# Two seven-product units on one NeuronCore: two of four weight sums of the second unit move from accumulating transfers to VectorE

## The chip, the core and the metric

The kernel runs on one core of a Trainium2 chip. The core has five engines that run side by side, each with its own queue of instructions worked off in order, and they wait for each other through semaphores. TensorE (PE in the profile) multiplies, with its weight loads shown apart as PEld. VectorE (DVE), ScalarE (ACT) and GpSimd (POOL) do elementwise work. SyncE (SP) only issues transfers here. Transfers are issued from SP's, ACT's and POOL's queues and carried by 16 DMA engines. The metric is the time of one execution in device microseconds (us); lower is better.

## The reference, cut to what matters

One decoder layer on 512 tokens with a model width of 1024: a layer norm, a token mixer (gated linear attention, called GLA, beside multi-head latent attention, called MLA), a merge by sigmoid gates, an output projection, and an MLP with hidden width 4096.

```python
h = layer_norm(x, ln_in_g, ln_in_b)
q_g, k_g, v_g, r_g, a_lr, q_lat, kv_lat, gate_logits = jnp.split(h @ w_in, offsets, axis=-1)
o_gla = gla_chunked(q_g, k_g, v_g, log_a)             # 4 heads, 256 values each
y_gla = (rms_norm(o_gla, gla_norm_g) * silu(r_g)) @ w_o_gla
y_mla = mla_causal_attention(...) @ w_o_mla           # 8 heads
g_gla, g_mla = split(sigmoid(gate_logits + b_gate))
h = layer_norm(ALPHA * h + (g_gla * y_gla + g_mla * y_mla) @ w_out, ln1_g, ln1_b)
out = layer_norm(ALPHA * h + square(relu(h @ w_ff1)) @ w_ff2, ln2_g, ln2_b)
```

The change lies in `v_g = h @ w_in[:, 1024:2048]` and `r_g = h @ w_in[:, 2048:3072]`, two products of 512x1024 by 1024x1024, and in the place where a GLA head's output is multiplied by silu of `r_g`.

## The kernel before

All products use float32 operands split in two parts, a high one (rounded to the type fp32r) and a low one (what is left), and each product of two blocks is three matmuls: high by high, high by low, low by high. A weight tile is split in `pump` (lines 165 to 189): ScalarE copies the raw tile into `whi` or `xh` (line 185), and VectorE subtracts that from the raw tile into `wlo` or `xl` (line 186). A table called `stream` lists every weight tile of the program in the order of use; `pump` keeps the transfers two tiles and the splits one or two tiles ahead of the product that TensorE is on. The pair `whi`/`wlo` has two buffers each, so a split into them waits until TensorE is done with the tile two uses earlier; `xh`/`xl` lie in a larger pool of 4 KB buffers (called A here).

The products for `r_g` and `v_g` are done by `unit` with seven products instead of eight. A 1024x1024 weight is cut in four blocks 11, 12, 21, 22 of 512x512. Seven products, here called phases 0 to 6, use the weights T1, 11, 22, T2, 21, T3 and T4, where T1 = 11 + 12, T2 = T1 + 22, T3 = 22 + 12 and T4 = T2 + 21 (signs are put on the other factor). The other factor is a block of `h`, or a sum of such blocks, called S1 to S4, which is computed once in the first unit (`r`), kept in device memory, and fetched again by POOL's queue for the second unit (`v`). Each phase has two half phases of 12 matmuls with a 512-wide right side, one for each tile of two rows of 128.

The four weight sums are made by transfers: `r_load` loads a block into a tile called `rw` (512 KB), and with `add` it issues a transfer from POOL's queue that adds another block onto the tile. T2 is added onto the tile of T1 once T1 has been split, and T4 onto T2 in the same way; T3 is added onto the tile of 22. `r_begin` issues T1's two loads and its two adds. For the unit `v` this is called from the middle of the unit `r`.

Between the matmuls of the units, small pieces of other work are woven in by `tick`: the GLA heads' decay levels (the tiles `M`, `qk`, `SD`, `tot`, `pr` and `qkp`; a head's `tot`, `pr` and `qkp` are made by POOL, and `tot` then passes through ScalarE before VectorE multiplies `qk` by it), and silu of the unit `r`'s result (`th` by ScalarE, then a multiply by VectorE at line 725, then a store `rd` to device memory). After the unit `v` come the gates' products (line 236 to 238), among which the GLA heads' outputs are made by `gla_out`; it fetches a head's part of silu(`r_g`) back as a tile `rg`.

The program's text gives priorities, not the final order: a scheduler of the framework puts each engine's instructions in an order of its own, by priority and by when it reckons each can start. So a moved call moves rows on several queues.

Of the kernel before, what the change touches and what calls it, by code (L numbers as in the profile page):

```python
# [52 lines left out]
def tile_hybrid_block(ctx: ExitStack, tc: tile.TileContext, I, out, dbg=None):  # L53
# [19 lines left out]
    def A(shape, dt=F32, n="a"):  # L73
        tag, bufs = ("C", 8) if n in TAG_C else (n, TAG_W[n]) if n in TAG_W else ("A", 24)
        return pa.tile(shape, dt, tag=tag, bufs=bufs, name=nm(n))
# [86 lines left out]
    def pump(i):  # L162
        while st["dma"] < min(len(stream), i + 1 + DMA_AHEAD):
            e = stream[st["dma"]]
            st["dma"] += 1
            if "src" in e:
                continue
            raw = A([P, e["nk"], T * 2 // e["nk"]], F32, "wraw")
            for sl, src, cw in e["dmas"]:
                dst = raw[:, sl, :e["n"]]  # L170
                if cw is not None:
                    dst = dst.rearrange("p (h c) -> p h c", c=cw)
                nc.sync.dma_start(dst, src)
            e["raw"] = raw
        while st["spl"] < min(len(stream), i + 2 + SPLIT_AHEAD):
            e = stream[st["spl"]]
            if st["spl"] > i + e.get("ahead", SPLIT_AHEAD) and not e["res"]:
                break
            nk, n = e["nk"], e["n"]
            hi, lo = [A([P, nk, T * 2 // nk], F32R, w) for w in HOME["a" if e["res"] else e.get("home", "w")]]  # L180
            raw = e["src"]() if "src" in e else e.pop("raw")
            with ExitStack() as gates:
                for g in st["gates"]:
                    gates.enter_context(tc.issue_after(g.ins))
                st["ins"] = act(hi[:, :nk, :n], raw[:, :nk, :n], AF.Copy)  # L185
                vtt(lo[:, :nk, :n], raw[:, :nk, :n], f(hi[:, :nk, :n]), op=ALU.subtract)  # L186
            st["gates"] = ()
            e["w"] = (hi, lo)
            st["spl"] += 1

# [101 lines left out]
    PL["k"] = plan("w_in", C_K, T)  # L292
    ORDER = (("r", 0), ("v", 0), ("g", 0), ("g", 2), ("qr", 0), ("g", 1), ("g", 3), ("qr", 1))

    RPH = ("T1", "11", "22", "T2", "21", "T3", "T4")
    RW = {}
    RAHEAD, RHOME = 2, {"r": "wawawawawawaww", "v": "wawawawawawaww"}
# [4 lines left out]
    for sec, i in ORDER:  # L302
        if sec in "rv":
            c0 = {"r": C_R, "v": C_V}[sec]
            for n, op in enumerate(RPH):
                for hf in range(2):
                    PL[sec, n, hf] = len(stream)
                    if op in ("11", "21"):
                        plan("w_in", c0, T, 4 * (op == "21") + 2 * hf, 4 * (op == "21") + 2 * hf + 2)
                    else:  # L310
                        stream.append({"src": lambda q=(sec, op, hf): RW[q], "nk": 2, "n": T, "res": False})
                    stream[-1].update(ahead=RAHEAD, home=RHOME[sec][2 * n + hf])
        elif sec == "g":
            PL["g", i // 2, i % 2] = plan("w_in", C_G + i * T, T)
        else:
            plan_qr(i)
# [299 lines left out]
    def r_begin(sec):  # L616
        for hf in range(2):
            r_load(sec, "T1", 0, 1, hf)
        r_add(sec, "T1", "T1", 0, 0)

    def r_add(sec, dst, src, i, j):
        for hf in range(2):
            RW[sec, dst, hf] = RW[sec, src, hf]
            r_load(sec, dst, i, j, hf, add=True)
# [8 lines left out]
    def fetch(name):  # L633
        RS[name] = [A([P, 4, 256], F32R, name) for _ in range(2)]
        for d, w in zip(KEPT[name], RS[name]):
            nc.gpsimd.dma_start(w, d)
# [63 lines left out]
    def unit(sec, nxt=None):  # L700
# [45 lines left out]
        for n in range(7):  # L746
            o = a if n in (1, 3, 5) else b
            for hf in range(2):
                pump(PL[sec, n, hf])
                for pp in range(2):  # L750
                    for t in range(2):
                        xh, xl = lhs(n, 2 * hf + pp, t)
                        hi, lo = [w[:, pp] for w in stream[PL[sec, n, hf]]["w"]]
                        opens = n in (0, 1, 4, 6) and hf == 0 and pp == 0
                        mm(o[t], xh, hi, start=opens, stop=False, skip_group_check=True)
                        mm(o[t], xh, lo, start=False, stop=False, skip_group_check=True)
                        mm(o[t], xl, hi, start=False, stop=hf == 1 and pp == 1, skip_group_check=True)
                if hf == 0 and (val or n in (0, 2, 4, 6)):
                    tick(None)
                if n == 0 and hf == 1:  # L760
                    r_add(sec, "T2", "T1", 1, 1)
                    if val:
                        fetch("S2")
                if n == 2 and hf == 1:
                    r_add(sec, "T3", "22", 0, 1)
                    if val:
                        fetch("S3")
                if n == 3 and hf == 1:
                    r_add(sec, "T4", "T2", 1, 0)
                if n == 5 and hf == 0 and nxt:  # L770
                    r_begin(nxt)
                    fetch("S1")
                    fetch("S4")
                if n == 6 and hf == 0 and nxt:
                    for h2 in range(2):
                        r_load(nxt, "22", 1, 1, h2)
            for t in range(2):
                if n == 0:
                    put("22", t, o[t], -1.0)
                elif n == 1:  # L780
                    put("11", t, o[t])
                elif n == 2:
                    put("12", t, o[t], -1.0)
                elif n == 3:
                    last("12", t, o[t], ALU.subtract)
                elif n == 4:
                    last("11", t, o[t], ALU.add)
                elif n == 5:
                    put("21", t, o[t])
                    last("22", t, o[t], ALU.subtract)  # L790
                else:
                    last("21", t, o[t], ALU.add)
            if n < 6:
                tick(None)
# [129 lines left out]
    def gla_out(h):  # L924
        while SS[h] is None or Vp[h // 2] is None or Rp[h // 2] is None:
            yield
        sd, s128, kq = SS[h]
        rg = A([P, NT, HV], F32, "rg")
        for i in range(2):
            nc.sync.dma_start(rg[:, 2 * i:2 * i + 2], Rp[h // 2][i][:, :, h % 2 * HV:(h % 2 + 1) * HV])  # L930

        def V(j):
            c = slice(h % 2 * HV, (h % 2 + 1) * HV)
# [12 lines left out]
        for i in range(NT):  # L946
# [12 lines left out]
                mm(o, al, bh, start=False, stop=n == len(todo) - 1)  # L959
            sq = B([P, HV], F32, "osq")  # L960
            act(sq, o, AF.Square, accum_out=ss[:, i:i + 1])
            if i >= 1:
                yield
        vts(ss, ss, 4.0 / HV, 4.0 * RMS_EPS, op0=ALU.mult, op1=ALU.add)
# [3 lines left out]
        og = [B([P, 2, HV], F32, "og") for _ in range(2)]  # L968
        for i in range(NT):
            o = ps[i // 2][:, (i % 2) * HV:(i % 2 + 1) * HV]  # L970
            stt(og[i // 2][:, i % 2, :], o, rs[:, i:i + 1], rg[:, i],
                op0=ALU.mult, op1=ALU.mult)
        yield
        for kk in range(2):
# [582 lines left out]
```

## Time and profile before

| What | Value |
| --- | --- |
| median of 3 runs | 883.69 us (883.59 to 885.77) |
| the profiled execution | 883.45 us, of which 881.7 us is the span from the first to the last instruction |
| mean granted TensorE clock | 0.994 |
| TensorE matmuls | 854.5 us busy, 97% of the span |
| VectorE, ScalarE, GpSimd | 69%, 53%, 21% busy |
| transfers | 127.35 MB, mean 144 GB/s |

A row of the profile that names a source line counts by the kernel before (L186 is line 186 of it). In a timeline, the bracket at a row's end says how long the engine was idle before it, and which engine or transfer ended that idle time. Rows of equal instructions that follow each other are merged, with their count. In a table of stretches, each engine's busy time stands with its instructions in brackets; "PEclk" is the granted clock as a share of full speed. Matmuls overlap: one with a 512-wide right side is shown with 0.39 us, while the next one starts 0.23 us after it.

### The profile page before, as it was taken

To read this page: it belongs to the slowest core of one execution; us is meant where nothing else is said; L and a number is where in the kernel's file an instruction comes from. 1 tells how busy PE (TensorE), PEld (TensorE's weight loads), DVE (VectorE), ACT (ScalarE), POOL (GpSimd) and SP (SyncE) were. 2 spreads that over 40 slices of the span, in tenths; PEclk is the share of its full clock that TensorE was granted. 3 is DMA by queue.
4 is the path that set the end of the run, shared out by engine and by line. 5 is a ranking of instruction groups with operands and counts; after the bars stand their busy time and mean duration, and the time that the engine had idled before them with its cause. 6 is when DMAs were issued, how large, how long until landed. Compare 5 with 4: busy or idle time off the path is not lost. (4 is left out here: it accounts for less than half of the span.)

```text
span 881.7 us, 11628 instructions
## 1 busy us (share of the span) xinstructions
PE 854.5 (97%) x4288; PEld 726.2 (82%) x4288; DVE 610.0 (69%) x993; ACT 466.2 (53%) x802; POOL 188.0 (21%) x221
## 2 busy tenths in 40 slices
PE   5999997999999999999999999999999999999995
PEld 5988785778898888888988888988888888888885
DVE  7977986796556344557876797886567556754697
ACT  5467765564554433435654414565457546735662
POOL 2404683603202010000000013004400520242023
PEclk9999998999999999999999999999999999999998
DMA  7836898933454223111307527006941990398075
GB/s 229 241 103 218 250 267 227 250 124 105 122 176 120 63 63 105 52 53 55 109 25 261 191 76 282 1 1 168 291 114 30 260 256 27 68 304 202 0 191 96
DMA packets 73240, 127.35 MB, mean 144 GB/s; under 512 B 8641, under 2 KB 34676, under 8 KB 73184
## 3 DMA queue, kind: packets, MB, share of 16 engines
q1 hardware_dynamic: 50848, 70.86, 24.8%
q0 software_dynamic: 20416, 52.11, 24.7%
q10 hardware_dynamic: 1920, 3.66, 1.2%
q8 instruction: 33, 0.54, 0.2%
q14 instruction: 23, 0.19, 0.1%
HBM read 99.86 MB, written 12.58 MB: 128 GB/s over the span
## 5 line engine op out<-in xcount | busy, mean ns | idle before, releaser
L186 DVE TENSOR_TENSOR wlo<-wraw,whi 128x1024 fp32r<-128x1024 f32 (+2 forms) x90 | 102.2, 1137 | 97.8 <-ACT whi L185 92.0
L236 PE MATMUL mm<-h,whi 128*128 128x512 f32 x416 | 163.2, 393 | 0.1
L237 PE MATMUL mm<-h,whi 128*128 128x512 f32 x416 | 162.8, 391 | 0.0
L238 PE MATMUL mm<-h,wlo 128*128 128x512 f32 x416 | 155.9, 391 | 0.1
L185 ACT ACTIVATE whi<-wraw 128x1024 fp32r<-128x1024 f32 (+2 forms) x90 | 87.0, 967 | 69.9 <-PE mm L237 34.5
L1419 POOL DMA_DIRECT2D res<-ev x54 | 47.8, 992 | 237.6 <-ACT ev L1417 194.2
L236 PEld LDWEIGHTS mm<-h,whi 128*128 128x128 f32 x416 | 78.2, 188 | 16.0 <-ACT whi L185 0.3
L238 PEld LDWEIGHTS mm<-h,wlo 128*128 128x128 f32 x416 | 77.9, 188 | 16.2 <-DVE wlo L186 0.5
L237 PEld LDWEIGHTS mm<-h,whi 128*128 128x128 f32 x416 | 78.2, 188 | 15.1
L1484 ACT ACTIVATE relu<-mm 128x512 f32<-128x512 f32 x32 | 18.8, 595 | 56.9 <-PE mm L238 56.9
L374 POOL TENSOR_TENSOR mv<-mv,mhalf 128x1 f32<-128x1 f32 x4 | 4.1, 1036 | 208.5 <-DVE mv L373 208.5
L185 ACT ACTIVATE xh<-wraw 128x1024 fp32r<-128x1024 f32 (+1 forms) x24 | 23.2, 974 | 26.8 <-PE mm L271 15.4
L614 POOL DMA_DIRECT2D rw<-in_w_in_dram x24 | 26.1, 1128 | 32.6 <-DVE xl L186 12.9
L186 DVE TENSOR_TENSOR wlo<-wq,whi 128x1024 fp32r<-128x1024 f32 x15 | 18.4, 1224 | 19.9 <-ACT whi L185 19.9
L856 ACT ACTIVATE M<-qk 128x256 f32<-128x256 f32 x56 | 23.9, 454 | 14.1 <-DVE qk L838 13.3
L186 DVE TENSOR_TENSOR xl<-wraw,xh 128x1024 fp32r<-128x1024 f32 (+1 forms) x24 | 27.0, 1137 | 6.3 <-ACT xh L185 6.3
L1417 ACT ACTIVATE ev<-mm 128x512 f32<-128x512 f32 x20 | 11.9, 600 | 31.6 <-DMA res<-ev 27.8
L838 DVE TENSOR_TENSOR qk<-qk,tot 128x512 f32<-128x512 f32 x28 | 23.5, 840 | 7.1 <-PE px L894 4.2
L1334 POOL DMA_DIRECT2D wq<-in_w_ff_dram x32 | 24.5, 1024 | 11.1 <-issue 4.6
L236 PE MATMUL mm<-ogT,whi 128*128 128x512 f32 x64 | 25.7, 401 | 0.0
L237 PE MATMUL mm<-ogT,whi 128*128 128x512 f32 x64 | 25.3, 395 | 0.0
L237 PE MATMUL mm<-omT,whi 128*128 128x512 f32 x64 | 25.2, 394 | 0.0
(457 smaller groups left out, 2413.6 us busy)
## 6 DMA issues: line engine op xcount, KB each, us to landing
wraw<-in_w_in_dram SPq DMA_DIRECT2D x32, 512.0 KB, 4.6
wraw<-in_w_ff_dram SPq DMA_DIRECT2D x32, 512.0 KB, 8.6
wq<-in_w_ff_dram POOLq DMA_DIRECT2D x32, 512.0 KB, 9.9
res<-ev POOLq DMA_DIRECT2D x54, 256.0 KB, 8.6
rw<-in_w_in_dram POOLq DMA_DIRECT2D x24, 512.0 KB, 7.7
S<-s SPq DMA_DIRECT2D x8, 512.0 KB, 6.4
S<-S POOLq DMA_DIRECT2D x8, 512.0 KB, 7.1
wraw<-in_w_o_gla_dram SPq DMA_DIRECT2D x8, 512.0 KB, 3.7
```

The source lines that it names most:

```text
L185: st["ins"] = act(hi[:, :nk, :n], raw[:, :nk, :n], AF.Copy)
L186: vtt(lo[:, :nk, :n], raw[:, :nk, :n], f(hi[:, :nk, :n]), op=ALU.subtract)
L236: mm(o, hi[:, c], xh, start=first, stop=False)
L237: mm(o, hi[:, c], xl, start=False, stop=False)
L238: mm(o, lo[:, c], xh, start=False, stop=last)
L614: nc.gpsimd.dma_start(RW[sec, op, hf], w[:, k0:k0 + 2, c0:c0 + T], **({"accum_op": ALU.add} if add else {}))
L838: vtt(new, new, view(tot, o + 1, -1, 2, 0, s), op=ALU.mult)
L856: act(packed(M, s, i), half_lr(qk, s, i), AF.Copy)
L1334: nc.gpsimd.dma_start(t, w2[:, k0:k0 + 3:2, j * T:(j + 1) * T])
L1417: st["ev"] = act(e, o, AF.Copy, scale=-1.0 if ph == 4 else 1.0)
L1419: nc.gpsimd.dma_start(res[tt + t][:, j * T:(j + 1) * T], e, accum_op=ALU.add)
L1484: act(r, ps, AF.Relu)
```

## The change

The unit `r` is left as it is. In the unit `v`, the sums T2 and T4 are no longer made by transfers that add onto the tile of T1. Instead `v_sum` lets VectorE add the raw tile of 22 onto the tile of T1, in place, right behind the split of 22, and the raw tile of 21 onto it right behind the split of 21. That is four additions of 128x1024 (two halves each), and four fewer accumulating transfers of 512 KB on POOL's queue. T1 = 11 + 12 and T3 = 22 + 12 are still made by transfers.

The start of the unit `v` (`r_begin`: two loads and two adds of T1) is called in phase 3 of the unit `r`, where it was called in phase 5. S1's fetch is called half a phase later than before, and S4's in phase 0 of the unit `v`, where it was called in phase 5 of the unit `r`.

In `gla_out`, silu(`r_g`) is fetched into two tiles of 2 KB a partition from another pool, after the head's third output block, where it was fetched into one tile of 4 KB ahead of all.

```diff
@@ pump @@
             st["gates"] = ()
+            if "then" in e:
+                e["then"](raw)
             e["w"] = (hi, lo)
@@ ahead of the stream of the two units @@
+    def v_sum(a, b, hf, raw):
+        t = RW["v", b, hf] = RW["v", a, hf]
+        vtt(t, t, raw, op=ALU.add)
+
@@ stream of the two units @@
                     stream[-1].update(ahead=RAHEAD, home=RHOME[sec][2 * n + hf])
+                    if sec == "v" and op in ("22", "21"):
+                        stream[-1]["then"] = lambda raw, a={"22": "T1", "21": "T2"}[op], b={"22": "T2", "21": "T4"}[op], hf=hf: v_sum(a, b, hf, raw)
@@ unit @@
                 if n == 0 and hf == 1:
-                    r_add(sec, "T2", "T1", 1, 1)
+                    if not val:
+                        r_add(sec, "T2", "T1", 1, 1)
                     if val:
                         fetch("S2")
...
-                if n == 3 and hf == 1:
+                if n == 3 and hf == 1 and not val:
                     r_add(sec, "T4", "T2", 1, 0)
-                if n == 5 and hf == 0 and nxt:
+                if n == 3 and hf == 0 and nxt:
                     r_begin(nxt)
+                if n == 5 and hf == 1 and nxt:
                     fetch("S1")
+                if n == 0 and hf == 0 and val:
                     fetch("S4")
@@ gla_out @@
-        rg = A([P, NT, HV], F32, "rg")
-        for i in range(2):
-            nc.sync.dma_start(rg[:, 2 * i:2 * i + 2], Rp[h // 2][i][:, :, h % 2 * HV:(h % 2 + 1) * HV])
...
+            if i == 2:
+                rg = []
+                for j in range(2):
+                    rg.append(B([P, 2, HV], F32, "rgb"))
+                    nc.sync.dma_start(rg[j], Rp[h // 2][j][:, :, h % 2 * HV:(h % 2 + 1) * HV])
...
-            stt(og[i // 2][:, i % 2, :], o, rs[:, i:i + 1], rg[:, i],
+            stt(og[i // 2][:, i % 2, :], o, rs[:, i:i + 1], rg[i // 2][:, i % 2],
```

What the scheduler makes of it is seen on two engines. The first is POOL, late in the unit `r`. In these rows of the kernel before, `qkp` and `tot` belong to GLA head 1, `rw_275_1396` and `rw_276_1398` are the two halves of the unit `v`'s T1, which appear first as loads and then as adds, and S1 and S4 are the fetches:

```order
L813 TENSOR_TENSOR tot_260_1309<-tot_260_1309 128x16
L813 TENSOR_TENSOR tot_260_1309<-tot_260_1309 128x8
L824 TENSOR_TENSOR qkp_263_1322<-pr_261_1319,qkp_262_1321 128x512
L813 TENSOR_TENSOR tot_260_1309<-tot_260_1309 128x4
L614 DMA rw_275_1396<-in_w_in_dram 128x2x512
L614 DMA rw_276_1398<-in_w_in_dram 128x2x512
L636 DMA S1_277_1402<-S1_136_714 128x1024
L636 DMA S1_278_1403<-S1_137_715 128x1024
L636 DMA S4_279_1406<-S4_167_876 128x1024
L636 DMA S4_280_1407<-S4_168_877 128x1024
L614 DMA rw_275_1396<-in_w_in_dram 128x2x512
L614 DMA rw_276_1398<-in_w_in_dram 128x2x512
```

The add onto the tile `rw_109_591`, the second half of the unit `r`'s own T4, stands three rows ahead of these. The same place of the same queue in the changed kernel, with `rw_257_1287` and `rw_258_1289` for the halves of the unit `v`'s T1:

```order
L832 TENSOR_TENSOR pr_263_1325<-qk_145_785 128x512
L622 DMA rw_257_1287<-in_w_in_dram 128x2x512
L622 DMA rw_258_1289<-in_w_in_dram 128x2x512
L824 TENSOR_TENSOR tot_262_1315<-tot_262_1315 128x128
L622 DMA rw_109_591<-in_w_in_dram 128x2x512
L835 TENSOR_TENSOR qkp_265_1328<-pr_263_1325,qkp_264_1327 128x512
L824 TENSOR_TENSOR tot_262_1315<-tot_262_1315 128x64
L622 DMA rw_257_1287<-in_w_in_dram 128x2x512
L622 DMA rw_258_1289<-in_w_in_dram 128x2x512
L644 DMA S1_279_1418<-S1_136_714 128x1024
L824 TENSOR_TENSOR tot_262_1315<-tot_262_1315 128x32
L644 DMA S1_280_1419<-S1_137_715 128x1024
```

T1's loads now stand right behind `pr`, ahead of the unit `r`'s last add, and T1's adds stand ahead of S1's fetch and of the last four `tot`.

The second engine is VectorE at the start of the unit `v`. Before, `rg` with `mm` is the unit `r`'s last sum, `wraw_304_1516` and `wraw_298_1487` are the halves of 11, `rw_290_1461` is the first half of 22, and the rest belongs to GLA heads 0 and 1 and to silu:

```order
L713 TENSOR_TENSOR rg_283_1426<-rg_283_1426,mm_209_1044 128x512
L186 TENSOR_TENSOR xl_306_1519<-wraw_304_1516,xh_305_1518 128x1024
L884 TENSOR_TENSOR SD_313_1564<-px_319_1590,ca_75 128x512
L725 SCALAR_TENSOR_TENSOR rg_237_1185<-th_322_1600,rg_237_1185 128x512
L186 TENSOR_TENSOR wlo_300_1490<-wraw_298_1487,whi_299_1489 128x1024
L112 TENSOR_TENSOR kq_288_1455<-px_287_1452,kq_288_1455 128x256
L112 TENSOR_TENSOR sd_301_1505<-px_302_1506,sd_301_1505 128x256
L838 TENSOR_TENSOR qk_145_785<-qk_145_785,tot_260_1309 128x2x128x2
L863 COPY_PREDICATED SD_313_1564<-cmask_87,px_320_1593 128x2x128
L186 TENSOR_TENSOR wlo_312_1549<-rw_290_1461,whi_311_1548 128x1024
```

The same stretch in the changed kernel, where the two rows of line 299 are the sums T2 (T1's tile plus the raw tile of 22):

```order
L721 TENSOR_TENSOR rg_281_1422<-rg_281_1422,mm_209_1044 128x512
L186 TENSOR_TENSOR xl_306_1519<-wraw_304_1516,xh_305_1518 128x1024
L299 TENSOR_TENSOR rw_258_1289<-rw_258_1289,rw_289_1459 128x1024
L895 TENSOR_TENSOR SD_313_1563<-px_319_1590,ca_75 128x512
L299 TENSOR_TENSOR rw_257_1287<-rw_257_1287,rw_288_1457 128x1024
L186 TENSOR_TENSOR wlo_298_1486<-wraw_296_1483,whi_297_1485 128x1024
L733 SCALAR_TENSOR_TENSOR rg_237_1185<-th_322_1600,rg_237_1185 128x512
L112 TENSOR_TENSOR kq_286_1451<-px_285_1448,kq_286_1451 128x256
L112 TENSOR_TENSOR sd_299_1501<-px_300_1502,sd_299_1501 128x256
L849 TENSOR_TENSOR qk_145_785<-qk_145_785,tot_262_1315 128x2x128x2
L186 TENSOR_TENSOR wlo_312_1547<-rw_288_1457,whi_311_1546 128x1024
```

Both sums of T2 now stand ahead of the split of the first half of 11. The sums of T4 stand in the same way ahead of the split of the first half of 21, three phases on. Behind the unit `v`, up to the gates' last product, rows of all engines trade places by a few, with no row added or taken away apart from the fetches' tiles; from the first product with `w_o_gla` on, the order is the same.

## The prediction

> **What bounds the kernel now.** I read the page's busy shares first, then the table of whom TensorE waited for, over the whole span.
>
> ```profile
> PE 854.5 (97%) x4288; PEld 726.2 (82%) x4288; DVE 610.0 (69%) x993; ACT 466.2 (53%) x802; POOL 188.0 (21%) x221
> ...
> PE px L389 <- DMA wraw<-in_w_in_dram: 8.8, 1, 8.8
> PE mm L755 <- ACT whi L185: 5.1, 1, 5.1
> PE mm L756 <- DVE wlo L186: 2.2, 2, 1.9
> ```
>
> TensorE is the bound, so only its idle time can be won. The 8.8 us are the first load of the program, which the change does not touch. The other two rows are lines 755 and 756, the matmuls of the seven-product units: 5.1 us once, and 2.2 us in two waits. Next I cut the span at these places, to see what surrounds them.
>
> ```profile
> 140.40:145.49 5.09, 0.00 (x0) 0.00 (x0) 0.96 (x1) 2.05 (x3) 0.00 (x0) 0.79 0.88 323
> 145.49:150.39 4.90, 4.67 (x10) 3.24 (x11) 4.90 (x8) 3.88 (x8) 4.55 (x5) 0.52 0.21 20
> ...
> 174.30:194.20 19.90, 19.69 (x97) 16.17 (x97) 19.33 (x32) 11.93 (x22) 3.42 (x6) 1.00 0.41 143
> ...
> 194.20:540.00 345.80, 345.70 (x1841) 296.51 (x1842) 218.90 (x428) 162.92 (x330) 32.84 (x40) 1.00 0.35 113
> 540.00:860.00 320.00, 319.65 (x1510) 268.48 (x1508) 217.96 (x270) 178.95 (x258) 66.42 (x80) 1.00 0.53 139
> ```
>
> The columns are the stretch and its length, then busy time and count of PE, PEld, DVE, ACT and POOL, the granted clock, the transfers' share and GB/s. Three things matter. Right behind the idle stretch the clock is 0.52, and only ten matmuls fit into 4.90 us. VectorE is busy for 19.33 of 19.90 us late in the unit `v`. And from 194.2 to 860 us TensorE is idle for 0.45 us in all, so whatever the unit `v` wins earlier reaches the end whole: nothing behind it waits for anything else.
>
> Now the chain that ends in the 5.1 us, from the timelines and, for the landings, the table of transfers in the two stretches where T1's loads and T1's adds are issued.
>
> ```profile
> 124.94 1.50 POOL L614 DMA_DIRECT2D rw<-in_w_in_dram  x2
> 129.77 4.07 POOL L614 DMA_DIRECT2D rw<-in_w_in_dram  x4 [1.15 <-DMA rw<-in_w_in_dram]
> ...
> rw<-in_w_in_dram POOLq DMA_DIRECT2D x2, 512.0 KB, 4.5
> ...
> rw<-in_w_in_dram POOLq DMA_DIRECT2D x2, 512.0 KB, 11.0
> ...
> 143.44 1.06 ACT L185 ACTIVATE xh<-rw 128x1024 fp32r<-128x1024 f32 x1 [6.98 <-DMA rw<-in_w_in_dram]
> ...
> 144.53 1.23 DVE L186 TENSOR_TENSOR xl<-rw,xh 128x1024 fp32r<-128x1024 f32 x1 [6.98 <-ACT xh L185]
> 145.67 1.22 DVE L186 TENSOR_TENSOR wlo<-rw,whi 128x1024 fp32r<-128x1024 f32 x1
> ...
> 145.49 1.22 PE L755 MATMUL mm<-whi,S 128*128 128x512 f32 x2 [5.11 <-ACT whi L185]
> 146.94 0.79 PE L756 MATMUL mm<-wlo,S 128*128 128x512 f32 x1 [0.23 <-DVE wlo L186]
> ```
>
> T1's loads leave at 124.9 and land in 4.5 us; the adds leave at 129.8 and take 11.0 us; ScalarE has waited 6.98 us when they land, and TensorE starts 5.11 us late. The second wait has another cause.
>
> ```profile
> 169.76 1.79 DVE L874 TENSOR_TENSOR qk<-qk,g 128x512 f32<-128x512 f32 x1
> 171.47 2.77 DVE L186 TENSOR_TENSOR wlo<-wraw,whi 128x1024 fp32r<-128x1024 f32 x1
> ...
> 171.43 1.72 POOL L824 TENSOR_TENSOR qkp<-pr,qkp 128x512 fp32r<-128x512 f32 x1
> ...
> 174.30 0.50 PE L756 MATMUL mm<-wlo,h 128*128 128x512 f32 x1 [1.95 <-DVE wlo L186]
> ```
>
> VectorE has no pause here; beside POOL's `qkp` a split of 2.77 us stands instead of 1.22 us, and TensorE waits 1.95 us for it.
>
> **What can be won.** 5.11 + 0.23 = 5.34 us of idle time before T1; 4.90 us for ten matmuls that take 2.3 us at full clock (0.23 us apart, as further on), less the 0.23 us already counted, = 2.37 us; and 1.95 us. Together 9.66 us.
>
> **T1's loads and adds, two phases sooner.** The moved call issues two loads and two adds. On POOL's queue the loads now come right behind `pr`, so they pass the last add of the unit `r`, `qkp` and six `tot`; the adds pass S1's fetch and four `tot`. SP's queue is not passed: its weight loads keep their order.
>
> ```profile
> 108.23 0.32 SPq L522 DMA_DIRECT2D latd<-latT  x1
> ...
> 113.55 1.74 POOL L821 TENSOR_TENSOR pr<-qk 128x512 f32<-128x512 f32 x1
> ...
> 117.88 1.21 POOL L614 DMA_DIRECT2D rw<-in_w_in_dram  x1 [1.78 <-DVE xl L186]
> ...
> 130.96 1.06 ACT L185 ACTIVATE whi<-rw 128x1024 fp32r<-128x1024 f32 x1 [3.74 <-issue]
> ...
> latd<-latT SPq DMA_DIRECT2D x1, 512.0 KB, 6.6
> ...
> DMA to landing us min/median/max: 4.1/7.7/13.4
> ...
> DMA to landing us min/median/max: 2.6/6.7/9.2
> ```
>
> (The last two rows are the landings of all tiles `rw` and of the fetched S1 to S4.) One T1 tile reuses a buffer from which `latd` was stored; that store is done at 108.23 + 6.6 = 114.8. `pr` ends at 113.55 + 1.74 = 115.3, so the loads leave at 115.3 to 116.8 instead of 124.94. At the median they land at 116.1 + 7.7 = 123.8, and the adds leave at about 123.8 to 125.3 instead of 129.77 (6 us earlier) and take the 11.0 us seen, 13.4 at most: T1 is there at 135 to 138, before TensorE wants it at 140.40. ScalarE's two splits are 1.06 us each and VectorE's 1.22 us, and nothing else stands ahead of them there (both sat idle 6.98 us), so the first low part is ready by about 140.6. I take the 5.34 us as won, with up to 1 us left in the bad case; and with no stall the half clock behind it, which stands only there, goes too.
>
> What is queued behind the waiting adds: S1's fetch and four `tot`. S1 leaves at about 126.5 and lands by 126.5 + 9.2 = 135.7, again before 140.40. `tot` ends at about 127.7; ScalarE's exponential of it stands ahead of the unit `r`'s last split (130.96), which TensorE does not need before about 134 if it is to have its low part at 137.7. So POOL has 6 us of slack. The unit `r`'s own last add stays at its 117.9.
>
> **S1 and S4 fetched later.** S4's fetch, before among the four of 126.44, waits for the unit `r`'s phase 5 (about 133) and lands by 142.2; TensorE reads it first in phase 2, about 146.5. Cost nothing, hidden behind phases 0 and 1.
>
> **Four sums by VectorE, four transfers fewer.** The sum in place has the shape of an addition further on in the kernel.
>
> ```profile
> L1342 DVE TENSOR_TENSOR wq<-wq,wq 128x1024 f32<-128x1024 f32 x8 | 9.8, 1225 | 6.3 <-DMA wq<-in_w_ff_dram 6.2
> ...
> 162.49 1.06 ACT L185 ACTIVATE whi<-rw 128x1024 fp32r<-128x1024 f32 x1 [6.23 <-DMA rw<-in_w_in_dram]
> ...
> 163.58 1.23 DVE L186 TENSOR_TENSOR wlo<-rw,whi 128x1024 fp32r<-128x1024 f32 x1 [5.92 <-ACT whi L185]
> ...
> 146.89:190.07 43.18, 36.88 (x47) 0.96 0.81 208
> ...
> 188.86 1.21 DVE L186 TENSOR_TENSOR wlo<-rw,whi 128x1024 fp32r<-128x1024 f32 x1
> ...
> 192.61 0.39 PE L757 MATMUL mm<-whi,h 128*128 128x512 f32 x1
> ```
>
> 1.225 us alone; back to back such a row costs 1.14 us (144.53 to 145.67), so four cost 4.56 us. Against them stands the pause of 5.92 us, in which ScalarE and VectorE waited for T2's accumulating transfer: nothing waits for a transfer there any more. The window from T1's split to that of T4's second half (columns: its length, VectorE's busy time, count) has 6.3 us idle, nearly all of it this pause.
>
> VectorE's chain to T4's last split ended at 188.86 + 1.21 = 190.07. Now: it starts at 140.6 instead of 145.67 + 1.22 = 146.89 (6.3 less), without the pause (5.92 less), with four sums (4.56 more), and one `vl` row that stood ahead of the split now stands behind it (0.60 less): 190.07 - 6.3 - 5.92 + 4.56 - 0.60 = 181.8. Ten matmuls follow, 2.3 us: 184.1. TensorE alone would be done at 192.61 + 0.23 - 9.66 = 183.2. So a new wait of 0.9 us is left. The price of a sum beside POOL no row shows; from below it is nothing, where a sum fills a pause, and from above 2.77 us, as the split beside `qkp`, 1.55 us more than alone. I take the price alone for the first two sums, since POOL has only short `sd` work near them (0.98 to 1.64 us), and 0.3 us more each for the two later ones, which come near POOL's `tot`, `pr` and `qkp`: a new wait of 1.5 us. In phase 4 the sums of T4 stand ahead of the split that was late before; by the same chain that split ends at about 160.5 and is wanted at 163.6, so the 1.95 us are won. POOL's four issues saved (1.2 us each) are worth nothing, as POOL is 21% busy.
>
> **Gates in two 2 KB tiles.** The fetch now comes behind three output blocks.
>
> ```profile
> 195.87 1.25 SPq L930 DMA_DIRECT2D rg<-rd  x2
> ...
> 213.78 1.65 DVE L971 SCALAR_TENSOR_TENSOR og<-px,grs,rg 128x256 f32<-128x256 f32 x4
> ...
> DMA to landing us min/median/max: 3.3/4.8/8.5
> ```
>
> It was issued 17.9 us ahead of its use and lands in 8.5 us at most, so 17.9 - 8.5 = 9.4 us of delay are free for this head; the gates' matmuls run on meanwhile. I cost it at nothing. If that cover is gone, VectorE waits at line 971, with the sums of the gates' products queued behind it.
>
> **Sum.** 9.66 - 1.5 = 8.16 us off the profiled 883.45: 875.3 us. The median of the runs shown is 883.69, 0.24 us above the profiled one, which I leave aside. With no new wait it is 873.8, and with TensorE's small waits late in the unit (0.21 us in 174.30 to 194.20) and elsewhere gone as well, 873.0.
>
> **Rivals.**
> 1. *VectorE becomes the bound.* All four sums meet POOL's work at the 2.77 us of the one split that did: 4 x 1.55 = 6.2 us more, a new wait of 0.9 + 6.2 = 7.1, gain 2.56: 880.9. For it: VectorE is busy 36.88 of 43.18 us. Against it: POOL is busy 18.20 of those 43.18 us, much of it issue of transfers, and in the trace one of the fourteen splits of the unit `v` was stretched like that. The Trainium skill ("SBUF — State Buffer", section "SBUF: two separate sides") says that a VectorE instruction with two SBUF inputs and a GpSimd one that reads SBUF take a port pair from each other for the whole instruction. The split at 171.47 beside `qkp` agrees; by that rule, and with `qkp`'s 1.72 us for each sum, the new wait would be 7.8 us and the time 881.6.
> 2. *The change does not do what it says.* T1's adds land no earlier, because the transfers compete with the unit `r`'s loads. Stall and half clock stay, only the 1.95 us go: 881.5. For it: the transfers run at 0.87 of their time in 120 to 130 us as it is (row below). Against it: T1 would have to lose all of the 6 us.
> 3. *POOL's queue blocks: slower.* The adds stand at the head of POOL's queue until the loads have landed, with `tot` behind them, and ScalarE's exponential of `tot` ahead of the unit `r`'s last split. Beyond 6 us of delay each further microsecond is one of TensorE's idle time. From 14 us of delay on it is slower than before; with 18 us (12 beyond) the time is 875.3 + 12 = 887.3. For it: POOL is nearly full there. Against it: even the slowest landing, 13.4 us, is 5.7 us above the median, which the slack just covers.
>
> ```profile
> 120.00:130.00 10.00, 10.00 (x50) 8.38 (x48) 10.00 (x13) 5.07 (x9) 8.69 (x12) 1.00 0.87 246
> ```
>
> **How the numbers follow.** Forecast 0.57, rival 1 0.17, rival 2 0.12, rival 3 0.14 (its like in other queues counted with it). 0.3%, about 2.65 us, is what a measurement can tell from no change: forecast and rival 1 (2.8 us, just beyond) are faster, together 0.74; rival 2 is the same, 0.12; rival 3 slower, 0.14. The likeliest alone has 873.0 to 878, where half of the four sums are stretched. The range reaches over rivals 1 and 2 to 882.6 and leaves out rival 3 and little else.
>
> **What would show it.** Right: T1's loads at 115 to 117, its adds before 126, no idle time of TensorE over 1 us at T1 and a granted clock near 1 in the ten matmuls behind; four VectorE additions of about 1.2 us, no pause of 5.9 us; the unit `v` ending 8 us earlier and the rest unchanged. Wrong: additions of 2 us and more with a wait of TensorE at T3 or T4 (rival 1); ScalarE still waiting for T1's transfer (rival 2); TensorE idle before 140 us at the unit `r`'s last weight (rival 3); a VectorE wait at line 971 for `rg`.

## The result

| | us |
| --- | --- |
| before, median of 4 runs | 883.64 (883.52 to 885.77) |
| changed, median of 4 runs | 872.86 (872.61 to 873.51) |
| ratio | 0.9874, interval 0.9856 to 0.9891 |
| profiled execution, span | 872.98, 871.2 (before 883.45, 881.7) |

The change makes the kernel 10.8 us faster, 1.3%. The direction and the place were as forecast, but 872.86 us lies 0.14 us below the range, which is less than the four runs differ among each other, and 2.4 us below the forecast of 875.3.

### The profile page after: what moved, and what is told of

The parts are those of the page before. It is cut to its first block, busy times and chain, and to the rows that moved or that the text cites. A ratio compares the mean times of both kernels' runs of the same rounds, so it can differ in the third digit from the quotient of the medians.

```text
span 871.2 us, 11627 instructions
## 1 busy us (share of the span) xinstructions
PE 851.2 (98%) x4288; PEld 725.8 (83%) x4288; DVE 607.9 (70%) x997; ACT 466.9 (54%) x802; POOL 180.9 (21%) x217
## 5 line engine op out<-in xcount | busy, mean ns | idle before, releaser
L186 DVE TENSOR_TENSOR wlo<-wraw,whi 128x1024 fp32r<-128x1024 f32 (+2 forms) x90 | 100.3, 1116 | 105.0 <-ACT whi L185 96.2
L622 POOL DMA_DIRECT2D rw<-in_w_in_dram x20 | 20.7, 1038 | 27.7 <-DVE xl L186 11.7
L849 DVE TENSOR_TENSOR qk<-qk,tot 128x512 f32<-128x512 f32 x28 | 21.4, 762 | 5.6 <-ACT M L867 5.3
```

What stands on the lines that cost most here:

```text
L622: nc.gpsimd.dma_start(RW[sec, op, hf], w[:, k0:k0 + 2, c0:c0 + T], **({"accum_op": ALU.add} if add else {}))
L849: vtt(new, new, view(tot, o + 1, -1, 2, 0, s), op=ALU.mult)
```

## The profile after

First the busy shares of the changed kernel and the table of whom TensorE waited for.

```profile
PE 851.2 (98%) x4288; PEld 725.8 (83%) x4288; DVE 607.9 (70%) x997; ACT 466.9 (54%) x802; POOL 180.9 (21%) x217
...
PE px L397 <- ACT x L386: 8.3, 1, 8.3
PE px L902 <- ACT M L867: 0.9, 1, 0.9
```

The waits of 5.1 us and 2.2 us at the matmuls of the two units are gone. Besides the first load's wait, one of 0.9 us is new: for `M`, a tile of the GLA heads' decay levels, made by ScalarE.

The stretches that answer to those of the prediction (same columns) show the unit `v`'s first matmuls, the new wait, and the rest of the program.

```profile
140.16:146.06 5.90, 5.90 (x29) 4.96 (x28) 5.90 (x8) 3.94 (x8) 1.71 (x3) 1.00 0.98 315
164.00:170.00 6.00, 5.11 (x27) 4.02 (x26) 4.31 (x7) 4.41 (x10) 3.66 (x5) 1.00 0.32 89
184.68:540.00 355.32, 355.29 (x1921) 306.38 (x1920) 226.94 (x449) 166.44 (x336) 32.91 (x43) 1.00 0.36 116
```

From 140.16 us TensorE never stops and the granted clock is 1.00, where it was 0.52. From the gates' first matmul to 540 us it is idle for 0.03 us.

Now T1's way through POOL, ScalarE and VectorE, from the timelines of the changed kernel.

```profile
115.62 1.51 POOL L622 DMA_DIRECT2D rw<-in_w_in_dram  x2
...
123.54 2.51 POOL L622 DMA_DIRECT2D rw<-in_w_in_dram  x2 [0.68 <-DMA rw<-in_w_in_dram]
...
136.16 1.06 ACT L185 ACTIVATE xh<-rw 128x1024 fp32r<-128x1024 f32 x1
...
138.99 1.22 DVE L186 TENSOR_TENSOR wlo<-rw,whi 128x1024 fp32r<-128x1024 f32 x1
...
142.46 1.22 DVE L299 TENSOR_TENSOR rw<-rw,rw 128x1024 f32<-128x1024 f32 x1
...
157.27 1.22 DVE L299 TENSOR_TENSOR rw<-rw,wraw 128x1024 f32<-128x1024 f32 x1
...
179.06 1.22 DVE L186 TENSOR_TENSOR wlo<-rw,whi 128x1024 fp32r<-128x1024 f32 x1
...
181.81 0.40 PE L764 MATMUL mm<-wlo,h 128*128 128x512 f32 x1
```

T1's loads leave at 115.6 and its adds at 123.5; ScalarE splits T1 at 136.16 without having waited for a transfer; the low part is ready at 138.99 + 1.22 = 140.2. The sums (line 299) take 1.22 us. T4's last split ends at 179.06 + 1.22 = 180.3; TensorE first reads it at 181.8.

How long both units take is read between two matmuls, the unit `r`'s first and the gates' first: before

```profile
94.87 0.47 PE L755 MATMUL mm<-whi,s 128*128 128x512 f32 x1 [0.60 <-ACT s L111]
...
194.15 0.50 PE L236 MATMUL mm<-h,whi 128*128 128x512 f32 x1
```

and in the changed kernel

```profile
95.28 0.47 PE L763 MATMUL mm<-whi,s 128*128 128x512 f32 x1 [0.60 <-ACT s L111]
...
184.68 0.40 PE L238 MATMUL mm<-h,whi 128*128 128x512 f32 x1
```

that is 99.28 us and 89.40 us: the units give 9.88 us. The span gives 10.5 us. The unit `r` began 0.41 us later in the changed kernel's profile (over the profiles it lies between 94.9 and 96.2 us, before anything that was changed), and what lies behind the gates' first matmul is about 1 us shorter: 0.45 us of it in the gates' first five matmuls, some 0.4 us in the gates' products behind them, and 0.2 us behind the last matmul. The length of both units, read like this, is given for each experiment below; where the scheduler moved rows past the gates' first matmul (the doubled sums), it tells less than the time.

## The experiments

Each kernel ran in four to six executions beside the kernel before on the same chip (median there 883.6 to 884.6 us).

| kernel | us | ratio to before, interval | both units, us |
| --- | --- | --- | --- |
| changed | 872.86 | 0.9874 (0.9856 to 0.9891) | 89.40 |
| early T1, later S1 and S4, sums by transfers | 872.41 | 0.9865 (0.9850 to 0.9881) | 88.23 |
| the same, gates in one tile | 872.19 | 0.9871 (0.9854 to 0.9887) | 88.22 |
| before, early T1 alone | 875.13 | 0.9898 (0.9882 to 0.9915) | 90.13 |
| sums by VectorE, T1 late | 880.59 | 0.9958 (0.9942 to 0.9974) | 97.44 |
| before, head 2's POOL work left out | 881.63 | 0.9970 (0.9959 to 0.9982) | 96.95 |
| changed, gates in one tile | 873.23 | 0.9877 (0.9861 to 0.9894) | 89.39 |
| changed, T1 in phase 4 | 874.54 | 0.9890 (0.9875 to 0.9905) | 90.90 |
| changed, T1 in phase 2 | 873.33 | 0.9886 (0.9871 to 0.9900) | 89.86 |
| changed, S3's fetch later | 872.55 | 0.9865 (0.9851 to 0.9880) | 88.54 |
| T2 by VectorE, T4 by transfers | 871.91 | 0.9869 (0.9854 to 0.9883) | 88.17 |
| changed, T2's sums doubled | 872.51 | 0.9878 (0.9864 to 0.9893) | 87.18 |
| changed, all four sums doubled | 880.75 | 0.9955 (0.9939 to 0.9970) | 90.16 |

### Which part brings the gain

Early T1, with the later fetches of S1 and S4, and the four sums left to transfers:

```diff
                 if n == 0 and hf == 1:
-                    if not val:
-                        r_add(sec, "T2", "T1", 1, 1)
+                    r_add(sec, "T2", "T1", 1, 1)
...
-                if n == 3 and hf == 1 and not val:
+                if n == 3 and hf == 1:
...
-                    if sec == "v" and op in ("22", "21"):
+                    if False:
```

> The changed kernel, with T2 and T4 of the unit v made by accumulating transfers again (as in the kernel before); T1 is still begun in phase 3, the gates still in two tiles. If the parts add up (theory A): the stall of 5.1 us at T1, its restart and the half clock go (together about 7.9 us by the spacing of the matmuls), the wait of 1.95 us for a VectorE split beside POOL's work stays: about 875.7. If the sums on VectorE are what lets T1 come in time (theory B: otherwise T2's transfers lie in front of T1's or of S1's on the same queue and engines), the stall comes back in part: 878 or more, with ScalarE waiting for a transfer at T1 or T2.

872.41 us: the whole gain, 3.3 us better than theory A and without the wait that theory B asks for. In its timelines stand

```profile
154.27 1.06 ACT L185 ACTIVATE whi<-rw 128x1024 fp32r<-128x1024 f32 x1 [0.41 <-DMA rw<-in_w_in_dram]
...
158.51 3.15 DVE L186 TENSOR_TENSOR wlo<-wraw,whi 128x1024 fp32r<-128x1024 f32 x1
```

The pause for T2's transfer is 0.41 us on ScalarE, where it was 6.23. The split beside POOL's work is even longer than before, 3.15 us instead of 2.77, and yet TensorE does not wait for it. An earlier T1 is split earlier, and so T2's adds onto it leave earlier too. So the second wait hangs on the first one, though an early T1 alone does not remove all of it, as a run further on shows.

The sums alone, with T1, S1 and S4 called in phase 5 as before:

```diff
-                if n == 3 and hf == 0 and nxt:
-                    r_begin(nxt)
-                if n == 5 and hf == 1 and nxt:
-                    fetch("S1")
-                if n == 0 and hf == 0 and val:
-                    fetch("S4")
+                if n == 5 and hf == 0 and nxt:
+                    r_begin(nxt)
+                    fetch("S1")
+                    fetch("S4")
```

> The changed kernel, with T1's loads and adds, S1's and S4's fetch called together in phase 5 of the unit r, as in the kernel before. Theory A: the stall and the half clock stay (about 7.9 us), the wait of 1.95 us goes and so do small waits behind the unit: 880 to 881.5. Theory B (the sums are the larger part): 876 to 878.

880.59 us, as theory A has it. TensorE's waits, and the stretch behind the first of them:

```profile
PE mm L763 <- ACT whi L185: 5.2, 1, 5.2
...
PE mm L764 <- DVE wlo L186: 0.2, 1, 0.2
...
146.12:152.00 5.88, 5.65 (x12) 3.97 (x13) 5.88 (x8) 3.87 (x8) 2.73 (x3) 0.50 0.47 151
```

The stall and the half clock stay, and the wait of 1.95 us goes. So the sums take away the second wait, and so does the early T1 with the later fetches; together they can't take it away twice.

The gates in one tile, once in the changed kernel and once in the kernel with early T1, later S1 and S4 and sums by transfers:

```diff
+        rg = A([P, NT, HV], F32, "rg")
+        for i in range(2):
+            nc.sync.dma_start(rg[:, 2 * i:2 * i + 2], Rp[h // 2][i][:, :, h % 2 * HV:(h % 2 + 1) * HV])
...
-            if i == 2:
-                rg = []
-                for j in range(2):
-                    rg.append(B([P, 2, HV], F32, "rgb"))
-                    nc.sync.dma_start(rg[j], Rp[h // 2][j][:, :, h % 2 * HV:(h % 2 + 1) * HV])
```

> The changed kernel, with silu fetched into one 4 KB tile ahead of all output blocks, as before. The span after the two units became about 1 us shorter, which no step of the prediction counted. If the gates' tiles give it: 873.9. If they are worth nothing, as the prediction has it: 872.9, within 0.4.

> T1 early with all four sums by transfers and S1 and S4 fetched later, but the gates again in one 4 KB tile (two parts of the change undone). If the gates' tiles are worth nothing: 872.4 as with the tiles. If the 2.7 us between the early T1 put into the kernel before (875.1) and T1 early in the changed kernel (872.4) come from the gates' tiles: about 875.

873.23 against 872.86, and 872.19 against 872.41: no difference that can be told, and the units' lengths agree within 0.01 us. The tiles are worth nothing.

The kernel before with one call moved:

```diff
-                if n == 5 and hf == 0 and nxt:
-                    r_begin(nxt)
-                    fetch("S1")
+                if n == 3 and hf == 0 and nxt:
+                    r_begin(nxt)
+                if n == 5 and hf == 0 and nxt:
+                    fetch("S1")
                     fetch("S4")
```

> The kernel before, with nothing changed but T1's loads and adds called in phase 3 of the unit r (S1 and S4 stay in phase 5, all four sums are transfers, the gates one tile). If the early T1 is the whole gain: 872.4, no wait of TensorE over 1 us in the unit v. If the later S1 and S4 or the gates' tiles are needed beside it: 875 or more, with a wait for a fetch or at the gates.

875.13 us: most of the gain, but not all. Its ScalarE, VectorE and TensorE in the timelines:

```profile
153.97 1.06 ACT L185 ACTIVATE whi<-rw 128x1024 fp32r<-128x1024 f32 x1 [4.99 <-DMA rw<-in_w_in_dram]
...
162.96 2.78 DVE L186 TENSOR_TENSOR wlo<-wraw,whi 128x1024 fp32r<-128x1024 f32 x1
...
165.79 0.50 PE L756 MATMUL mm<-wlo,h 128*128 128x512 f32 x1 [0.95 <-DVE wlo L186]
```

The second wait is back at half its size. This kernel differs from the one with sums by transfers and one tile for the gates (872.19) in where S1 and S4 are fetched, and with it in the order that the scheduler gives T2's halves. That other kernel shows in ScalarE's timeline

```profile
152.07 1.05 ACT L185 ACTIVATE xh<-rw 128x1024 fp32r<-128x1024 f32 x1
...
153.86 1.06 ACT L185 ACTIVATE whi<-rw 128x1024 fp32r<-128x1024 f32 x1 [0.25 <-DMA rw<-in_w_in_dram]
```

There the half whose add left first (138.87 us) is split first; in the kernel with 875.13 us the half whose add left second (142.12 us) stands first in ScalarE's queue, as in the kernel before, and ScalarE waits 4.99 us for it. That half lands no later: ScalarE's wait for it ends at 153.97 us here and at 153.86 us there. So the later fetches brought 2 to 3 us here (1.9 by the units' length, 2.4 by the ratios, 2.9 by the medians), and what differs at the wait is the order that came with them. The order was not changed by itself. Whether S1's or S4's place matters was not separated, and the changed kernel, with its sums by VectorE, was not run without the later fetches.

The kernel before has such an order at T1 as well. These are its two adds of T1, each by itself in the table of transfers, and a row of ScalarE's timeline.

```profile
rw<-in_w_in_dram POOLq DMA_DIRECT2D x1, 512.0 KB, 9.7
rw<-in_w_in_dram POOLq DMA_DIRECT2D x1, 512.0 KB, 12.3
...
144.40 1.04 ACT L185 ACTIVATE whi<-rw 128x1024 fp32r<-128x1024 f32 x1
```

The half that TensorE uses first (the one split into `whi`) has the first add: it left at 129.77 us and landed 9.7 us later, at 139.5, before TensorE stopped at 140.40. ScalarE split it only at 144.40, behind the other half, for whose add it waited until 143.44. So by the trace much of the 5.1 us stall hangs on the order of these two splits, and not on T1's lateness alone. No run changed this order alone, so what that would have won stays open.

### What the second wait needed

In the kernel before, head 2's work on POOL is replaced by copies on ScalarE:

```diff
-            gtt(src, a[:, :, 0], a[:, :, 1], op=ALU.add)
+            if h == 2:
+                act(src, a[:, :, 0], AF.Copy)
+            else:
+                gtt(src, a[:, :, 0], a[:, :, 1], op=ALU.add)
```

and likewise `pr` and the low part of `qkp`.

> The kernel before, with head 2's tot, pr and qkp not computed by POOL but replaced by copies on ScalarE (the sums and the products of that head are left out, so its output is not the reference's). T1 and T2 come as late as before. If the second wait (1.95 us) needs POOL's work beside VectorE's splits: the split is 1.22 us and the wait goes, 881.3 to 881.9. If the 5.92 us pause for T2 alone makes it: a wait of 1 us or more stays, 882.8 or more.

881.63 us. VectorE's timeline:

```profile
164.55 1.23 DVE L186 TENSOR_TENSOR wlo<-rw,whi 128x1024 fp32r<-128x1024 f32 x1 [5.79 <-ACT whi L185]
...
170.00 1.23 DVE L186 TENSOR_TENSOR wlo<-wraw,whi 128x1024 fp32r<-128x1024 f32 x1 [0.96 <-ACT whi L185]
```

The pause for T2 is still there, the late split takes 1.23 us instead of 2.77, and TensorE does not wait. So the wait of 1.95 us needed both, T2's lateness and POOL's work beside VectorE: it goes without POOL's work here, and without the pause for T2 in the kernels with 872.41 and 880.59 us.

### How early T1 has to be

```diff
-                if n == 3 and hf == 0 and nxt:
+                if n == 4 and hf == 0 and nxt:
                     r_begin(nxt)
```

> The changed kernel, with T1 begun in phase 4 instead of 3, so that its adds leave about 1 to 3 us later on POOL's queue and stand behind S1's first half. If T1 has several microseconds to spare in the changed kernel: 872.9, no wait at T1. If it comes just in time: a wait at T1 of 1 to 3 us and half clock behind it, 875 to 878.

> The changed kernel, with T1 begun in phase 2 of the unit r, one phase sooner still. If T1 already comes early enough in phase 3: 872.9. If POOL's queue blocks when T1's adds wait at its head (the prediction's slower rival): TensorE idles at the unit r's last weight sum, T4, or ScalarE waits for it; 875 or more.

Phase 4: 874.54 us. The adds leave at 126.8 and 129.5, and the timelines of ScalarE and TensorE show

```profile
137.59 1.06 ACT L185 ACTIVATE xh<-rw 128x1024 fp32r<-128x1024 f32 x1 [1.38 <-DMA rw<-in_w_in_dram]
...
141.70 0.50 PE L764 MATMUL mm<-wlo,S 128*128 128x512 f32 x1 [0.52 <-DVE wlo L186]
...
169.42 0.71 PE L902 MATMUL px<-M 128*128 128x128 f32 x4 [1.38 <-ACT M L867]
```

The time lies between the two that were expected. T1 comes 1.4 us late for ScalarE; TensorE waits 0.52 us for the low part, and no half clock follows. Phase 2: 873.33 us, the units 0.46 us longer than with phase 3. POOL's queue and then ScalarE's:

```profile
123.86 1.22 POOL L622 DMA_DIRECT2D rw<-in_w_in_dram  x1 [3.58 <-DMA rw<-in_w_in_dram]
...
131.32 0.63 ACT L828 ACTIVATE tot<-tot 128x508 f32<-128x508 f32 x1 [4.95 <-POOL tot L824]
131.86 1.04 ACT L185 ACTIVATE whi<-rw 128x1024 fp32r<-128x1024 f32 x1
```

Here the chain of the prediction's slower rival can be seen: an add waits 3.58 us at the head of POOL's queue, `tot` behind it is late, ScalarE waits 4.95 us for it, and the unit `r`'s last split stands behind that. But it is split at 131.9 us, before the 134 us that the prediction gave as the limit, and TensorE does not stop there. Phase 3 is early enough, and earlier wins nothing.

### What the sums cost

All four sums doubled, and T2's alone:

```diff
         vtt(t, t, raw, op=ALU.add)
+        vtt(t, t, t, op=ALU.max)
```

> The changed kernel, with a second VectorE pass of the same size over the tile behind each of the four sums (maximum of the tile with itself, which changes no value): 4 x 1.14 = 4.56 us more of VectorE. If VectorE's chain sets the end of the unit v, as the prediction reckoned, each microsecond goes through: about 877. If that chain has slack (3.45 us idle in it and 1.5 us at its end in the changed kernel): 873 to 874.5.

> The changed kernel with the second VectorE pass behind T2's two sums alone: 2.28 us more of VectorE. All four doubled cost 7.9 us for 4.56. If VectorE's time costs in proportion: 876.8. If there is slack first and the cost comes when GLA levels slip out of the unit v into the gates' products: 873 to 874.5.

2.28 us more of VectorE cost nothing (872.51), 4.56 us more cost 7.9 us (880.75). Neither of the two theories holds over both: there is slack first, and then more than one to one. The two kernels differ in the place of the added time as well as in its amount, as only the dearer one has it behind T4's sums; the two were not separated. The doubled kernel's waits of TensorE, and two stretches of it:

```profile
PE px L903 <- ACT M L868: 1.7, 2, 1.2
...
PE px L903 <- ACT ogT L114: 1.2, 1, 1.2
PE mm L764 <- DVE rg L722: 0.8, 1, 0.8
...
140.00:200.00 60.00, 57.52 (x277) 47.39 (x276) 55.23 (x72) 35.91 (x63) 19.45 (x17) 1.00 0.54 164
200.00:540.00 340.00, 336.64 (x1798) 288.67 (x1797) 212.60 (x423) 159.29 (x324) 31.27 (x40) 1.00 0.35 112
```

The two units take only 0.76 us longer than in the changed kernel. The rest, about 6 us, is behind them: between 200 and 540 us TensorE is idle for 3.36 us, and it waits for `ogT` and `M` of the GLA heads, which now come late among the gates' products, where in the changed kernel nothing waited. What else is lost there was not traced one by one; some of it is matmuls of the GLA heads that have moved there out of the units.

T2 by VectorE, T4 by transfers:

```diff
-                    if sec == "v" and op in ("22", "21"):
+                    if sec == "v" and op == "22":
...
-                if n == 3 and hf == 1 and not val:
+                if n == 3 and hf == 1:
```

> The changed kernel with T2 summed by VectorE and T4 by accumulating transfers onto that tile. If VectorE's sums cost by their time (two instead of four, 2.3 us less of VectorE): the wait of 0.89 us for M shrinks or goes, 872.0 to 872.5. If the wait comes from S3's fetch ahead of head 2's tot on POOL, which stays: 872.9. If T4's transfers come late: a wait at T4, 874 or more.

871.91 us, without the wait for `M`, about as the first theory has it; but the next section finds this wait tied to an order of rows. It is the lowest time of all, but its interval and those of the changed kernel and of early T1 alone lie over each other: no version here beats the changed kernel by more than can be told.

### Where the new wait for M comes from

S3's fetch one phase later:

```diff
                     r_add(sec, "T3", "22", 0, 1)
-                    if val:
-                        fetch("S3")
...
+                if n == 3 and hf == 1 and val:
+                    fetch("S3")
```

> The changed kernel, with S3's fetch called one phase later, so that on POOL's queue it no longer stands ahead of head 2's tot and pr. If TensorE's new wait of 0.89 us (for M) comes from tot held up behind S3's fetch, which waits for a store: the wait goes, 871.7 to 872.0. If it comes from the 4.56 us of sums on VectorE: the wait stays, 872.9.

872.55 us, and the wait is gone, but not as expected. In the changed kernel POOL, ScalarE and TensorE show

```profile
158.05 3.25 POOL L824 TENSOR_TENSOR tot<-g 128x256 f32<-128x256 f32 x1
...
166.70 0.63 ACT L828 ACTIVATE tot<-tot 128x508 f32<-128x508 f32 x1 [1.35 <-POOL tot L824]
167.24 0.71 ACT L867 ACTIVATE M<-qk 128x256 f32<-128x256 f32 x2
...
168.00 0.71 PE L902 MATMUL px<-M 128*128 128x128 f32 x4 [0.89 <-ACT M L867]
```

and with S3's fetch later, in ScalarE's timeline

```profile
162.82 0.73 ACT L867 ACTIVATE M<-qk 128x256 f32<-128x256 f32 x2
...
166.96 0.63 ACT L828 ACTIVATE tot<-tot 128x508 f32<-128x508 f32 x1 [2.89 <-POOL tot L824]
```

`tot` is begun 5 us sooner (153.3), but is done no sooner: its exponential is at 166.96 instead of 166.70. What changed is ScalarE's order. In the changed kernel the exponential of head 2's `tot` stands ahead of head 1's `M`, so `M` waits for POOL; here `M` stands ahead. The changed kernel with the gates in one tile, with T1 in phase 4 and with T1 in phase 2 have the same order and the wait (0.88, 1.38 and 1.28 us), and so has the one with all four sums doubled (1.24 us); the kernels with early T1 and sums by transfers, with T2 alone summed by VectorE, with T2's sums doubled and with S3's fetch later have `M` first and no such wait. In the kernel with the sums alone the exponential stands between the two rows of that `M`, and TensorE does not wait either. So S3's fetch is not the cause by way of `tot`, as that theory had it, and VectorE's 4.56 us alone are not the cause either: what goes with the wait is one place in ScalarE's order. That order was not changed by itself.

## Why the prediction was right or wrong

Two steps failed. The term "what can be won" was too small (9.66 us; 10.9 by the spacing of the matmuls). And the parts of the change were given the wrong shares: the 1.95 us of the second wait were put down to the sums alone, where an earlier T1 with later fetches wins them without the sums, and the later fetches were costed at nothing.

**The stall at T1 and the half clock: right.** T1's adds left 6.2 us earlier (123.5; forecast 123.8), the low part was ready at 140.2 (forecast 140.6), and the clock stayed at 1.00. What the prediction did not see is that in the kernel before the half of T1 that TensorE needs first had landed by 139.5 us and stood behind the other half in ScalarE's queue.

**"What can be won": too small.** This is the largest of the differences that put the time outside the range. It counted the idle time ahead of a matmul and the ten slow matmuls behind T1, 9.66 us. By the spacing of the matmul starts over 0.23 us, T1's stall with the slow matmuls behind it cost 7.9 us and the second wait 2.3 us, and the matmuls that TensorE begins slowly after a pause and small waits of 0.1 to 0.3 us another 0.7: 10.9 us. The range's lower end, 873.0, left room for 0.8 us beyond the 9.66, and only with no new wait at all.

**The new wait of 1.5 us: near in size by luck, wrong in cause.** The chain of VectorE was to end at 181.8 and hold TensorE up by 0.9 us and more. It ended at 180.3, 1.5 us before it was wanted. The sums cost 1.22 us each, near the price alone that the prediction took (1.14 us back to back, with 0.3 us more each for the two later ones). Two groups of VectorE rows between T1's and T4's last split show what was not reckoned with: before

```profile
L838 DVE TENSOR_TENSOR qk<-qk,tot 128x512 f32<-128x512 f32 x7 | 6.5, 922 | 0.0
...
L186 DVE TENSOR_TENSOR wlo<-wraw,whi 128x1024 fp32r<-128x1024 f32 x2 | 4.0, 1992 | 0.0
```

and in the changed kernel

```profile
L849 DVE TENSOR_TENSOR qk<-qk,tot 128x512 f32<-128x512 f32 x7 | 4.8, 688 | 1.4 <-ACT M L867 1.4
...
L186 DVE TENSOR_TENSOR wlo<-wraw,whi 128x1024 fp32r<-128x1024 f32 x2 | 2.4, 1221 | 0.0
```

The window that answers to the prediction's (its length, VectorE's busy time and count) is

```profile
140.21:180.28 40.07, 36.62 (x51) 1.00 0.63 187
```

The rows of these two groups got 3.3 us shorter, since they no longer stretch beside POOL's work; of the pauses 40.07 - 36.62 = 3.45 us are left, where the forecast left 0.4. What did come is the 0.89 us for `M`, about 1.1 us by spacing, from ScalarE's order, which the prediction did not look at.

**Where the gain comes from: wrong in part.** The prediction gave the 1.95 us to the sums. Early T1 with later fetches and transfers for all sums wins it as well. T1's early start and the later fetches of S1 and S4 are enough for the whole gain; the fetches, costed at nothing, were worth 2 to 3 us beside an early T1 with sums by transfers. The four sums by VectorE win 1.8 us of the units' length where T1 is late (99.28 to 97.44) and nothing measurable where it is early: there the units are 1.2 us longer with them (89.40 against 88.23), which is about the wait for `M`, and the times can't be told apart.

**POOL's issues, gates in two tiles: right,** nothing.

**The sum.** Against the profiled runs the gain was 883.45 - 872.98 = 10.5 us, forecast 8.16. Of the 2.3 us between them 1.3 are "what can be won", 0.4 the smaller new wait, and some 0.6 lie outside the two units (about 1 us won behind them, 0.4 lost in the start of the program).

**The rivals.** VectorE as the bound did not come, but is not far: 2.3 us more behind T2's sums are free, 4.6 us more behind all four are not. T1 no earlier in effect: no. POOL's queue blocking: its chain was seen with T1 in phase 2, inside the slack.

## What to carry to other kernels

When two waits of the bounding engine follow each other on one chain of buffers, ask whether the second is there because of the first, before pricing separate cures: here an earlier start of one load removed the first and half of the second, and with the order that two later fetches brought, all of it. Measure what a stall costs from the start-to-start times of the matmuls behind it, since the idle time in a list of waits leaves out the slow restart. And where a scheduler sets the order, a moved call may be worth what it does to the order of other rows; look for a row that waits for another engine or a transfer and stands ahead of one that need not.

## What the runs showed of the hardware

After an idle stretch of 5.1 to 5.2 us the granted clock was 0.52 and 0.50 over the next 5 to 6 us, with matmuls 0.43 us apart instead of 0.23. After short waits it did not fall: the 1.95 us before were followed by 1.00 (the stretch from 174.30 us in the prediction), and these are the stretches of the kernel with T1 in phase 4 that begin with the wait of 0.52 us and hold the one of 1.38 us.

```profile
140.47:146.00 5.53, 5.01 (x24) 3.85 (x23) 5.53 (x8) 4.62 (x8) 2.84 (x3) 1.00 0.96 326
169.00:175.00 6.00, 5.58 (x28) 4.76 (x29) 5.60 (x11) 5.59 (x11) 0.32 (x1) 1.00 0.26 101
```

The Trainium skill ("TensorE: Matmul & The Clock Gate", section "Part 1: The HAM clock gate (the "warmup" mystery)") puts the array at half clock after at least one idle window of about 3.4 us and back at full clock after at least one busy window of about the same length; its windows run freely. The runs agree on the first (1.95 us no, 5.1 us yes). The slow matmuls lasted from 145.5 to 150.3 us before and from 146.1 to 152.0 us with the sums alone, longer than one such window and shorter than two.

POOL's work stretches VectorE's rows: with head 2's POOL work left out every split of the unit `v` takes 1.22 to 1.26 us. Which side pays changes with the order. Before, POOL's first `tot` of head 2 was short and a VectorE split took 2.77 us; in the changed kernel the sum and the split beside `tot` kept their 1.22 us and `tot` took 3.25 us (shown above). This is that `tot` before:

```profile
165.86 1.57 POOL L813 TENSOR_TENSOR tot<-g 128x256 f32<-128x256 f32 x1
```

With S3's fetch later a sum paid, 2.55 us, near the 2.77 us that the prediction gave as the price from above.

```profile
158.19 2.55 DVE L299 TENSOR_TENSOR rw<-rw,wraw 128x1024 f32<-128x1024 f32 x1
```
